# The low half of the FFN's gate and up weights by an adding DMA instead of a VectorE subtraction

## The chip, the cores and the metric

The kernel runs on one core of a Trainium2 chip. The metric is the time of one launch on the device, in microseconds (us). The matrix engine is called PE, the vector engine DVE, the scalar engine ACT, the GpSimd engine POOL and the sync engine SP. SP issues nearly all of the DMAs; POOL issues a few, on a queue of its own.

## The reference

Two layers over 512 tokens of 1024 features, in float32. Each layer has three attention mixers, a gated merge and an output projection, and then the part that the change touches, a SwiGLU feed-forward network (FFN) with 2816 hidden features:

```python
for l in range(DEPTH):
    mod = (cond @ w_ada[l] + b_ada[l]).reshape(b, 6, d)
    ...
    u = rms_norm(x, g_ffn[l]) * (1 + sc_f) + sh_f
    h = jax.nn.silu(u @ w_ffn_gate[l]) * (u @ w_ffn_up[l])
    x = x + gt_f * (h @ w_ffn_down[l])
return rms_norm(x, g_final)
```

`mod` is the modulation: six vectors per layer that come from the condition and the matrix `w_ada`.

## The kernel before

**Products in two halves.** Each float32 operand of a large product is cut into hi, which is the value rounded to the format of PE's faster products (`F32R`), and lo, which is the value minus hi. `mm3` then makes three matmuls: hi times hi, hi of the weight times lo of the activations, and lo of the weight times hi of the activations (lines 199, 200 and 201). A weight tile of 128 x 1024 holds eight chunks of 128 columns, so one unit of the FFN's first products is 24 matmuls of 128 x 512.

**The weights' way.** `LOADS` lists all weight tiles in the order of their use. `load` (line 150) fetches one into a buffer `wraw` by a DMA from SP; there are four of these buffers. `divide` makes `wh` by ACT (line 171) and `wl` by DVE (line 173). `W` hands PE its unit, lets `divide` run three units ahead of it and `fetch` four in the FFN. There are three buffers each for `wh` and `wl`, and from the output projection to the end of the FFN a fourth (tag `x`). A `wraw` buffer can be loaded anew when the last instruction that reads it is through.

**The first products of the FFN** ("gu" units: gate and up in turn, 44 tiles a layer). The first three units are computed together in half the tokens and then in the other half (PSUM tiles `f`), since the norm of the second half comes later. After that each pass `f` has one gate unit (PSUM tile `fg`, three banks) and one up unit (`fu`, two banks), and then ACT makes `g` = silu(`fg`), DVE multiplies it by `fu` (line 894), ACT rounds that to `hh` (line 243) and DVE makes `hl` (line 244).

**The modulation in the background.** In layer 0's FFN each pass also works on two columns of the next layer's modulation: `background(2)` calls `ada` twice, and each loads 512 KB of `w_ada` into a `wraw` buffer, the same four that the weights use, and reduces it on DVE (line 372). Layer 1's FFN has none of this.

**Order.** PE issues in the order in which the program is written; the order on ACT, DVE, POOL and SP is made by a scheduler when the kernel is built, and each engine then works strictly in that order. SP's queue is one of them: a DMA that must wait for its buffer holds up all that stand behind it.

Of the kernel before, what the change touches and what calls it, by code (L numbers as in the profile page):

```python
# [17 lines left out]
P = 128  # L18
# [14 lines left out]
# columns of the constants  # L33
C_INV, C_SGN, C_N = 0, 1, 2
# columns of the small vectors of a layer
# [4 lines left out]
# the blocks of queries whose weights ScalarE normalises  # L40
SCALE_ACT = {"f": (3,), "m": (2, 3)}
# between steps of the products: scores of a head (c), and transposes and products of the head before (p)
# [8 lines left out]
# products of constants that keep TensorE's clock up at the start  # L51
WARM = (24, 12)
# steps of products before each norm of the latents
WAIT = (8, 3, 8, 4)
# the chunk after which the rope tables are made
ROPE_AT = 4
# the chunk of the first products of the FFN after which the second half's norm comes
SS_AT = 3
# how far the work of attention goes before other work in the schedule, and steps by which the weights' division waits
HP, LAG = 30, 1  # L60

# 2*pi in parts of 8 bits, so that a product with a whole number below 2**16 is exact
# [4 lines left out]
def tile_hybrid_trunk(ctx: ExitStack, tc: tile.TileContext, xT, cvec, pos, cst, cmask, vec, gfin,  # L67
# [19 lines left out]
    # TensorE issues in the order written here; the other engines as the scheduler finds best  # L87
    ctx.enter_context(tc.manual_schedule(engines={pe.engine}))

    # ScalarE's functions, in phases of one table set each  # L90
# [15 lines left out]
    def windows(l):  # L106
        """Units of matrix products to run beside the attention of a pair of heads."""
        fox = [[("proj", l, 3 * p + i) for i in range(3)] for p in range(4)]
        sb = [[("proj", l, 12 + 3 * p + i) for i in range(3)] for p in range(4)]
        mla = [[("uqr", l, p // 2)] * (p % 2 == 0) + [("uq", l, p), ("ukv", l, p)] for p in range(4)]  # L110
        mg = [("merge", l, b, m) for b in range(3) for m in range(KC)]
        w = fox + [mla[0], mla[1] + [sb[0][0]], mla[2] + [sb[0][1]], mla[3] + [sb[1][0]], [sb[0][2], sb[1][1]]]
        w.append([mg[0], sb[1][2], mg[1], mg[2]])
        for p in range(2, 4):
            w.append([u for i in range(3) for u in (mg[3 * p - 3 + i], sb[p][i])])
        return w + [mg[9:14], mg[14:16], mg[16:]]
# [42 lines left out]
    def divide(want, after=None):  # L159
        """hi and lo of the weights before the want-th; after: what goes before them on ScalarE and VectorE"""  # L160
        while len(splits) < min(want, len(LOADS)):
            j = len(splits)
            fetch(j + 1)
            c = LOADS[j][2]
            p_, tag = wp, ""
            if fourth[0]:
                fourth[1] += 1
                if fourth[1] % 4 == 1:
                    p_, tag = fourth[0], "x"
            wh = p_.tile([P, D], F32R, tag="wh" + tag, name="wh")  # L170
            ins = [act.copy(wh[:, :c], raws[j][:, :c]).ins]  # L171
            wl = p_.tile([P, D], F32R, tag="wl" + tag, name="wl")
            ins.append(dve.tensor_sub(wl[:, :c], raws[j][:, :c], wh[:, :c].bitcast(F32)).ins)  # L173
            for i, a in zip(ins, after or ()):
                tc.add_manual_dep(i, a.name, order, reason="more urgent")
            splits.append((wh, wl))

    def W(unit, n=1, raw=3, ready=2, lag=0):
        """The next n weights, of that unit on, as (hi, lo); later ones are on their way."""
        i = at[0]  # L180
        if fourth[0]:
            raw, ready = 4, 3
        assert LOADS[i][0] == unit, (LOADS[i][0], unit)
        at[0] = i + n
        divide(i + n)

        def ahead():
            divide(i + max(n, ready + 1))
            fetch(i + max(n, raw + 1))

        if lag:
            later(lag, ahead)
        else:
            ahead()
        return splits[i] if n == 1 else splits[i : i + n]

# [6 lines left out]
    def gemm(o, wt, acts, m=P, start=True, stop=True, c0=0, cols=FULL):  # L203
        """o += W^T a over the chunks of acts, in steps; wt = (hi, lo) holds them m columns each from c0 on."""
        wh, wl = wt
        n = len(acts)
        for k, (ah, al) in enumerate(acts):
            cs = slice(c0 + k * m, c0 + (k + 1) * m)
            mm3(o, wh[:, cs], wl[:, cs], ah[:, cols], al[:, cols], start and k == 0, stop and k == n - 1)
            if k < n - 1:  # L210
                yield
# [12 lines left out]
    def steps(n):  # L224
        """n steps of the products in the queue"""
        for _ in range(n):
            while queue:
                try:
                    next(queue[0])
                    break  # L230
                except StopIteration:
                    queue.pop(0)
            else:
                return
            tick()
# [14 lines left out]
    H = S // 2  # L250

    class Norm:
        """1/sqrt(mean of squares over the features) of half the tokens, in every partition."""
# [77 lines left out]
    make_identity(nc, identf)  # L331
    # additive masks of the diagonal block: a query sees keys <= it, and keys < it
# [9 lines left out]
    # rope tables, rows alike in each 32: cos, and -sin | +sin  # L342
# [9 lines left out]
    # sin: +-r; cos: sin(pi/2 - |r|)  # L352
# [10 lines left out]
    def ada(l, i, c, wt=None, on_pool=False, after=None):  # L363
        """Column c of part i of the modulation."""
# [12 lines left out]
        if i in (1, 4):  # L377
            # g * (1 + scale)
            s1, g0 = (s1a, V_GM) if i == 1 else (s1f, V_GF)
            dve.scalar_tensor_tensor(s1[l][:, c : c + 1], m, 1.0, vecs[:, l, g0 + c : g0 + c + 1], ALU.add, ALU.mult)  # L380
# [14 lines left out]
    # ================= layers =================  # L395
    def values(ap, psv, name, got):
        """[2 heads' features, tokens] in PSUM -> [keys, block, head, hi | lo of the features]."""
# [14 lines left out]
    class Head:  # L412
# [4 lines left out]
        def S(self, i):  # L417
# [8 lines left out]
            if self.kind == "s":  # L426
                # sigmoid(z) of the key times the product of sigmoid(-z) over the later keys
# [20 lines left out]
        def T(self, js):  # L448
            """The weights of key blocks js, keys on the partitions, as hi and lo."""
# [12 lines left out]
        def PV(self, j):  # L462
            """[64 features, queries] += values^T weights^T; rows 0-63: hi of the values, rows 64-127: lo."""
# [12 lines left out]
    def slot(cur, prev, n):  # L476
        """The scores of a head and the rest of the head before it, between n steps of the queue."""
# [13 lines left out]
    for l in range(L):  # L491
# [32 lines left out]
        if l == 0:  # L524
# [4 lines left out]
            def warm(n):  # L529
                """Products of constants while there is nothing else: TensorE's clock falls when it idles."""  # L530
# [5 lines left out]
            # room that has no other use yet  # L536
# [65 lines left out]
        # of a head: qa = its queries' hi and lo, ka = its keys' hi twice; kb = its keys' lo  # L602
# [80 lines left out]
        def latent_keys(pr):  # L683
            """The rows that are alike in all heads"""
# [57 lines left out]
        def merge(u, b, m):  # L742
            """merged[m] += sigmoid(gate) * (y_b w_o)"""
# [32 lines left out]
        # the first pair's projections, with the forget gates and the norms of the latents  # L776
        enqueue(0)
        steps(1)
        with scoped(f"fg{l}", "right") as lp:
            # log of the forget gates: min(z, 0) - ln(1 + exp(-|z|)); its sums, negated  # L780
# [183 lines left out]
def _inputs(x, c, positions, g_mix, w_ada, b_ada, w_in, b_fox_f, g_mla_q, w_mla_uq, g_mla_kv,  # L964
            w_mla_ukv, w_o_fox, w_o_mla, w_o_sb, w_out, g_ffn, w_ffn_gate, w_ffn_up, w_ffn_down, g_final):
    """The arrays of the launch: the inputs, laid out for it."""
# [5 lines left out]
    def tiles(w):  # L972
        # [L, K, N] -> [L, N / 128, 128 rows of a chunk, chunks, 128]
# [6 lines left out]
    def col(v):  # L980
        # [L, n * 128] -> [128, L, n]
        return v.reshape(v.shape[0], -1, P).transpose(2, 0, 1)
# [5 lines left out]
    def qkv(w):  # L988
        # q, k, v tiles of a pair of heads, pair after pair
# [9 lines left out]
    # l kc p quad head part 32 -> l quad p part kc head 32  # L999
    uqr = uqr.reshape(L, 3, P, 2, 4, 2, 32).transpose(0, 3, 2, 5, 1, 4, 6).reshape(L, 2, P, 768)  # L1000
    ukv = np.asarray(w_mla_ukv).reshape(L, 2, P, 4, 2, 2, 64)  # l kc p pair head k|v 64
    ukv = ukv.transpose(0, 3, 2, 5, 1, 4, 6).reshape(L, 4, P, 512)

    wo = np.stack([np.asarray(w_o_fox), np.asarray(w_o_mla), np.asarray(w_o_sb)], axis=1)  # L 3 512 1024
# [15 lines left out]
    # row i: queries of the first half of block i; keys of its second half  # L1020
# [25 lines left out]
# 10000 ** (-i / 16) in float32  # L1046
# [25 lines left out]
```

## Time and profile before

| what | us |
|---|---|
| median of 2 runs | 1899.68 (1897.41 and 1901.94) |
| span of the profiled execution | 1895.3 |
| PE busy | 1857.2 |
| DVE busy | 1169.2 |
| ACT busy | 852.1 |
| POOL busy | 141.8 |

The span runs from the first to the last instruction of one profiled execution, and what the metric adds to it is the start and the end of the launch: here the median of the runs lies 4.4 us above it. Layer 0's first FFN products run from about 595 to 841 us of the span, layer 1's from about 1521 to 1764 us. "Busy" of PE is modelled from pipelined matmuls, so 98% busy is not a PE at its peak, but idle time of PE that the profile shows is real.

### The profile page before, as it was taken

The page shows a single profiled execution, that of the slowest core. Times are in us where ns is not written, and L with a number is a line of the kernel's source. Part 1 is how long each engine was busy: PE and PEld are TensorE (multiplying, and loading weights), DVE is VectorE, ACT ScalarE, POOL GpSimd, SP SyncE. Part 2 cuts the span into 40 slices and gives each one's busy share as a digit, 9 for nine tenths or more (in the row PEclk, how much of TensorE's full clock was granted, in tenths as well). Part 3 has the DMA queues.
Part 4 walks back from the last instruction along what each step waited for, and adds up shares of the span by engine and source line. Part 5 has one row for each costly group of instructions (what it writes and reads, how often), then busy time and mean ns, then how long its engine had stood idle before and what let it go on. Part 6 is the DMA issues. An engine that isn't in the chain of part 4 may idle for free.

```text
span 1895.3 us, 24083 instructions
## 1 busy us (share of the span) xinstructions
PE 1857.2 (98%) x8956; PEld 1515.1 (80%) x8956; DVE 1169.2 (62%) x2043; ACT 852.1 (45%) x1543; POOL 141.8 (7%) x260
## 2 busy tenths in 40 slices
PE   6999999999999999999999999999999999999998
PEld 4788787777889888778897887777788888888887
DVE  8888887677756655554558898666664463333333
ACT  4767874443334322232237688544433342232321
POOL 4122100001000000000002121000110000000000
PEclk8999999999999999999999999999999999999999
DMA  7423323333642655555633222122142222223231
GB/s 276 141 73 81 82 79 117 102 110 131 208 150 70 211 177 184 171 184 194 197 107 101 66 68 85 66 84 83 68 145 99 97 100 100 95 95 98 92 92 53
DMA packets 76741, 224.22 MB, mean 118 GB/s; under 512 B 10768, under 2 KB 13968, under 8 KB 76624
## 3 DMA queue, kind: packets, MB, share of 16 engines
q1 hardware_dynamic: 69136, 213.30, 33.8%
q0 software_dynamic: 7488, 9.38, 2.5%
q8 instruction: 71, 1.16, 0.3%
q14 instruction: 46, 0.38, 0.1%
HBM read 209.20 MB, written 4.19 MB: 113 GB/s over the span
## 4 chain that ended last, share of the span: by engine, by line
PE 79%; DMA 9%; DVE 7%; issue 3%; ACT 2%; SPq 0%; DVEq 0%; POOL 0%; POOLq 0%
DMA wraw<-in_w_ada_dram 8%; PE gate L199 5%; PE gate L201 5%; PE gate L200 5%; PE proj L199 4%; PE proj L200 4%; PE dn L200 4%; PE dn L199 4%; PE dn L201 4%; PE proj L201 4%; PE o L199 3%; PE o L200 2%; PE o L201 2%; PE fu L200 2%; PE fu L199 2%
## 5 line engine op out<-in xcount | busy, mean ns | idle before, releaser
L171 ACT CAST wh<-wraw 128x1024 fp32r<-128x1024 f32 (+4 forms) x332 | 311.4, 939 | 560.3 <-PE fu L200 125.1
L173 DVE TENSOR_TENSOR wl<-wraw,wh 128x1024 fp32r<-128x1024 f32 (+4 forms) x332 | 375.8, 1132 | 230.0 <-ACT wh L171 224.7
L372 DVE CUSTOM_DVE_ANT_0 wraw<-wraw,condb 128x1024 f32<-128x1024 f32 x80 | 98.6, 1232 | 153.0 <-DMA wraw<-in_w_ada_dram 152.9
L199 PE MATMUL proj<-uh,wh 128*128 128x512 f32 x384 | 162.2, 422 | 0.0
L199 PE MATMUL gate<-uh,wh 128*128 128x512 f32 x384 | 157.8, 411 | 0.0
L201 PE MATMUL proj<-uh,wl 128*128 128x512 f32 x384 | 151.3, 394 | 0.0
L200 PE MATMUL proj<-ul,wh 128*128 128x512 f32 x384 | 151.3, 394 | 0.0
L201 PE MATMUL gate<-uh,wl 128*128 128x512 f32 x384 | 150.6, 392 | 0.0
L200 PE MATMUL gate<-ul,wh 128*128 128x512 f32 x384 | 150.6, 392 | 0.0
L199 PE MATMUL dn<-hh,wh 128*128 128x512 f32 (+1 forms) x396 | 145.5, 367 | 0.0
L200 PE MATMUL dn<-hl,wh 128*128 128x512 f32 (+1 forms) x396 | 145.4, 367 | 0.0
L201 PE MATMUL dn<-hh,wl 128*128 128x512 f32 (+1 forms) x396 | 144.4, 365 | 0.1
L201 PE MATMUL fu<-uh,wl 128*128 128x512 f32 x336 | 131.5, 391 | 1.6 <-DVE wl L173 1.6
L200 PE MATMUL fu<-ul,wh 128*128 128x512 f32 x336 | 131.0, 390 | 0.0
L199 PE MATMUL fu<-uh,wh 128*128 128x512 f32 x336 | 130.9, 389 | 0.0
L199 PE MATMUL fg<-uh,wh 128*128 128x512 f32 x320 | 125.5, 392 | 0.0
L200 PE MATMUL fg<-ul,wh 128*128 128x512 f32 x320 | 125.5, 392 | 0.0
L201 PE MATMUL fg<-uh,wl 128*128 128x512 f32 x320 | 125.5, 392 | 0.0
L199 PEld LDWEIGHTS gate<-uh,wh 128*128 128x128 f32 x384 | 72.0, 188 | 19.8 <-issue 4.8
L201 PEld LDWEIGHTS proj<-uh,wl 128*128 128x128 f32 x384 | 72.3, 188 | 16.9
L201 PEld LDWEIGHTS gate<-uh,wl 128*128 128x128 f32 x384 | 72.0, 188 | 16.7
L201 PEld LDWEIGHTS dn<-hh,wl 128*128 128x128 f32 x396 | 74.4, 188 | 13.3 <-DVE wl L173 0.5
(370 smaller groups left out, 3973.2 us busy)
## 6 DMA issues: line engine op xcount, KB each, us to landing
wraw<-in_w_proj_dram SPq DMA_DIRECT2D x96, 512.0 KB, 3.5
wraw<-in_w_gu_dram SPq DMA_DIRECT2D x88, 512.0 KB, 3.6
wraw<-in_w_ada_dram SPq DMA_DIRECT2D x80, 512.0 KB, 3.3
wraw<-in_w_dn_dram SPq DMA_DIRECT2D x32, 512.0 KB, 4.0
wraw<-in_w_o_dram SPq DMA_DIRECT2D x48, 256.0 KB, 2.6
wada<-in_w_ada_dram SPq DMA_DIRECT2D x16, 512.0 KB, 5.6
wraw<-in_w_out_dram SPq DMA_DIRECT2D x16, 512.0 KB, 3.5
wraw<-in_w_dn_dram SPq DMA_DIRECT2D x16, 384.0 KB, 3.1
```

The lines of the kernel that those rows point to most:

```text
L171: ins = [act.copy(wh[:, :c], raws[j][:, :c]).ins]
L173: ins.append(dve.tensor_sub(wl[:, :c], raws[j][:, :c], wh[:, :c].bitcast(F32)).ins)
L199: pe.matmul(o, wh, ah, start=start, stop=False)
L200: pe.matmul(o, wh, al, start=False, stop=False)
L201: pe.matmul(o, wl, ah, start=False, stop=stop)
L372: ins = dve.tensor_tensor_reduce(out=wt, in0=wt, in1=condb, op0=ALU.mult, op1=ALU.add, scale=1.0, scalar=0.0, accum_out=m).ins
```

## The change

For "gu" units alone, `wl` is no longer a subtraction on DVE. ACT writes minus the rounded weight into `wl` (a copy with scale -1, which rounds as the copy to `wh` does), and then a DMA issued from POOL adds the raw weight to what stands in `wl`. All other weights keep DVE's subtraction. Comments are taken out as well, which shifts lines behind the change by five.

```diff
             wl = p_.tile([P, D], F32R, tag="wl" + tag, name="wl")
-            ins.append(dve.tensor_sub(wl[:, :c], raws[j][:, :c], wh[:, :c].bitcast(F32)).ins)
+            if LOADS[j][0][0] == "gu":
+
+                act.activation(wl[:, :c], raws[j][:, :c], AF.Copy, scale=-1.0)
+                pool.dma_start(out=wl[:, :c], in_=raws[j][:, :c], accum_op=ALU.add)
+            else:
+                ins.append(dve.tensor_sub(wl[:, :c], raws[j][:, :c], wh[:, :c].bitcast(F32)).ins)
             for i, a in zip(ins, after or ()):
```

The scheduler also moves other instructions. On DVE, in layer 0's FFN, one pass stands like this before, from one multiplication of `g` to the next; `wraw...condb` is the reduction of a column of the modulation:

```order
L894 TENSOR_TENSOR g_6540<-g_6540,fu_6507 128x512
L372 ISA wraw_6624,mod1_81<-wraw_6624,condb_69 128x1024
L372 ISA mod1_81 128x1
L244 TENSOR_TENSOR hl6_6539<-g_6540,hh6_6538 128x512
L173 TENSOR_TENSOR wl_6558<-wraw_6512,wh_6556 128x1024
L376 TENSOR_TENSOR mod1_81<-mod1_81,vecs_70 128x1
L380 SCALAR_TENSOR_TENSOR s1a1_83<-mod1_81,vecs_70 128x1
L372 ISA wraw_6629,mod1_81<-wraw_6629,condb_69 128x1024
L372 ISA mod1_81 128x1
L173 TENSOR_TENSOR wl_6589<-wraw_6560,wh_6587 128x1024
```

The same pass on DVE now (the lines of the kernel are five higher):

```order
L899 TENSOR_TENSOR g_6557<-g_6557,fu_6523 128x512
L249 TENSOR_TENSOR hl6_6556<-g_6557,hh6_6555 128x512
L377 ISA wraw_6643,mod1_81<-wraw_6643,condb_69 128x1024
L377 ISA mod1_81 128x1
L381 TENSOR_TENSOR mod1_81<-mod1_81,vecs_70 128x1
L385 SCALAR_TENSOR_TENSOR s1a1_83<-mod1_81,vecs_70 128x1
L377 ISA wraw_6648,mod1_81<-wraw_6648,condb_69 128x1024
L377 ISA mod1_81 128x1
```

The two subtractions are gone, and `hl` stands ahead of both reductions instead of between them.

SP's queue has the same DMAs in the same order, gate, up and two columns of the modulation in each pass, but waits for other things. Before (what stands in brackets is awaited: `DVE` and `Activation` for an instruction of that engine, `DMAHW` for a DMA from SP):

```order
L150 DMA wraw_6560<-in_w_gu_dram 128x1024 [waits DMAHW6_49,DVE_49,Activation_49]
L150 DMA wraw_6591<-in_w_gu_dram 128x1024 [waits DVE_49]
L150 DMA wraw_6624<-in_w_ada_dram 128x1024 [waits DMAHW7_49,DMAHW1_49,DVE_49]
L150 DMA wraw_6629<-in_w_ada_dram 128x1024 [waits DMAHW0_49,DVE_49]
L150 DMA wraw_6639<-in_w_gu_dram 128x1024 [waits DMAHW2_49,DVE_49,Activation_49]
```

And now (`DMASW` is a DMA from POOL, here an adding one):

```order
L150 DMA wraw_6578<-in_w_gu_dram 128x1024 [waits DMAHW6_49,DMASW5_49,Activation_49]
L150 DMA wraw_6610<-in_w_gu_dram 128x1024 [waits DVE_49]
L150 DMA wraw_6643<-in_w_ada_dram 128x1024 [waits DMAHW1_49,DMAHW7_49,DMASW6_49,Activation_49]
L150 DMA wraw_6648<-in_w_ada_dram 128x1024 [waits DMAHW0_49,DVE_49]
L150 DMA wraw_6659<-in_w_gu_dram 128x1024 [waits DMAHW2_49,DMASW7_49,Activation_49]
```

The gate's load and the first column's load of each pass now wait for an adding DMA where they waited for a subtraction; the other two wait for a reduction on DVE as before.

On ACT, at the start of the first products, the units behind the first stand like this before (`sq` belongs to the norm, `uh` are the modulated activations):

```order
L171 CAST wh_5898<-wraw_5678 128x1024
L260 ACTIVATE sqnf0b_5798<-x1_2_4948 128x256
L285 ACTIVATE uh0_86<-v_5863,mod0_80 128x256
L285 ACTIVATE uh1_87<-v_5867,mod0_80 128x256
L171 CAST wh_5904<-wraw_5902 128x1024
L260 ACTIVATE sqnf0b_5827<-x1_3_4949 128x256
L285 ACTIVATE uh2_88<-v_5871,mod0_80 128x256
L285 ACTIVATE uh3_89<-v_5875,mod0_80 128x256
L171 CAST wh_5910<-wraw_5908 128x1024
```

And now:

```order
L171 CAST wh_5899<-wraw_5679 128x1024
L265 ACTIVATE sqnf0b_5799<-x1_2_4948 128x256
L290 ACTIVATE uh0_86<-v_5864,mod0_80 128x256
L290 ACTIVATE uh1_87<-v_5868,mod0_80 128x256
L175 ACTIVATE wl_5901<-wraw_5679 128x1024
L171 CAST wh_5906<-wraw_5904 128x1024
L265 ACTIVATE sqnf0b_5828<-x1_3_4949 128x256
L290 ACTIVATE uh2_88<-v_5872,mod0_80 128x256
L290 ACTIVATE uh3_89<-v_5876,mod0_80 128x256
L175 ACTIVATE wl_5908<-wraw_5904 128x1024
L171 CAST wh_5913<-wraw_5911 128x1024
```

Each unit has the second copy (line 175) behind its first one, with two `uh` between them.

## The prediction

> **What bounds the kernel now.** I read the page's first part, then the windows of the two stretches in which the change acts, then waits and chain there.
>
> ```profile
> span 1895.3 us, 24083 instructions
> PE 1857.2 (98%) x8956; PEld 1515.1 (80%) x8956; DVE 1169.2 (62%) x2043; ACT 852.1 (45%) x1543; POOL 141.8 (7%) x260
> ```
>
> PE bounds the kernel: it is idle for 1895.3 - 1857.2 = 38 us in all, so no relief of DVE can bring more than that, and what it brings must be PE idle time in the FFN. Windows of layer 0's first products, and of layer 1's:
>
> ```profile
> 630.00:700.00 70.00, 70.00 (x308) 57.42 (x307) 38.41 (x69) 19.88 (x26) 0.00 (x0) 1.00 0.56 186
> 1600.00:1700.00 100.00, 100.00 (x439) 82.08 (x438) 34.71 (x38) 29.38 (x38) 0.00 (x0) 1.00 0.27 95
> ```
>
> The columns are span of the window, busy PE, weight load, DVE, ACT, POOL, granted clock, DMA share and GB/s. In layer 1, 439 matmuls take 100 us, so a pass of 48 takes PE 48 x 100 / 439 = 10.93 us (a unit 5.47). PE has no idle time in either window, at full clock. What waits in layer 0 (microseconds in total, times, longest):
>
> ```profile
> DVE wraw L372 <- DMA wraw<-in_w_ada_dram: 97.4, 37, 5.5
> ...
> ACT wh L171 <- PE fu L200: 45.8, 14, 3.9
> ...
> PE fu L201 <- DVE wl L173: 1.6, 4, 0.7
> ```
>
> PE waits 1.6 us for the subtraction that the change removes, so that is about the whole prize there. But DVE waits 97.4 us for columns of the modulation, and the chain (start, duration, what) and SP's queue show why:
>
> ```profile
> 710.18 4.61 DMA wraw<-in_w_ada_dram
> ...
> 714.92 1.23 DVE wraw L372
> ...
> 716.18 3.13 DMA wraw<-in_w_ada_dram
> ...
> 720.49 1.22 DVE L173 TENSOR_TENSOR wl<-wraw,wh 128x1024 fp32r<-128x1024 f32 x1
> 720.60 0.33 SPq L150 DMA_DIRECT2D wraw<-in_w_gu_dram  x1
> 721.74 0.33 SPq L150 DMA_DIRECT2D wraw<-in_w_ada_dram  x1
> ```
>
> Four `wraw` buffers carry four loads a pass, and make a ring: column 1 lands, is reduced, column 2 takes its buffer, lands at 719.3, is reduced, frees the up unit's load (720.60), and column 1 of the next pass goes out when the subtraction that ends at 721.7 frees its buffer. One turn is 721.74 - 710.18 = 11.56 us, longer than PE's 10.93. DVE works in order, so `g` falls behind PE:
>
> ```profile
> 640.53 0.69 DVE L894 TENSOR_TENSOR g<-g,fu 128x512 f32<-128x512 f32 x1 [2.04 <-PE fu L201]
> ...
> 839.77 0.69 DVE L894 TENSOR_TENSOR g<-g,fu 128x512 f32<-128x512 f32 x1
> 840.86 0.40 PE L199 MATMUL dn<-hh,wh 128*128 128x512 f32 x1
> ```
>
> At 640 DVE still waits for PE; the multiplication at 839.77 belongs to the pass that PE ended one pass before 840.86, at 829.9, and is 9.9 us late. PE feels lateness only at 16.4 us: `fu` has two banks, so the up unit of pass f+2 needs the multiplication of pass f, and starts 10.93 + 5.47 us after that pass ended. The kernel before ends the stage just inside this room.
>
> **The change, part by part.** Removed: 88 subtractions of 1.22 us on DVE, of which PE waited for next to nothing. Added: 88 copies of 1.05 us on ACT (as the cast below), which is busy 19.88 of 70 us there, so they cost only where PE waits for the weight. And 88 adding DMAs of 512 KB on POOL's queue; POOL is busy 0.00 there, so nothing stands before them. PE's wait moves from DVE to that DMA, and the buffer is held until it lands.
>
> *The price of an adding DMA.* The trace has none. The nearest rows are the shares of the two queues and two kinds of DMA (KB, median us to landing):
>
> ```profile
> q1 hardware_dynamic: 69136, 213.30, 33.8%
> q0 software_dynamic: 7488, 9.38, 2.5%
> wraw<-in_w_gu_dram SPq DMA_DIRECT2D x88, 512.0 KB, 3.6
> t<-t POOLq DMA_DIRECT2D x32, 128.0 KB, 2.3
> ```
>
> For 512 KB (0.524 MB) a load of SP occupies the 16 engines 0.338 x 1895.3 x 0.524 / 213.3 = 1.57 us, a copy of POOL's queue 0.025 x 1895.3 x 0.524 / 9.38 = 2.65 us. An addition reads two operands for one write. The lower bound is a load's 1.57 us, the upper twice POOL's copy, 5.3 us; I take twice a load, 3.15 us, which also lies nearest POOL's own copy. A POOL copy of 128 KB lands in 2.3 us, of which 2.65 / 4 = 0.66 is engine time, so 1.64 is fixed: an adding DMA lands in 1.64 + 3.15 = 4.8 us (bounds 3.2 and 6.9) after its copy on ACT.
>
> The Trainium skill, page "Collectives: The Full Stack", Part 3, says that a reduce in the DMA engines costs two source reads and no more, so about half of 31 GB/s an engine. For 32 KB an engine that is an estimate of 2.1 us; by it the sum below would be about 20 us and the change within 2%. No run here shows an adding DMA yet; this trace's loads (1.57 us) run near 21 GB/s an engine, slower than the page's 31.
>
> *The start of the first products, both layers.* PE needs three units at once, in buffers that it frees only as the output projection ends:
>
> ```profile
> 589.59 1.03 ACT L171 CAST wh<-wraw 128x1024 fp32r<-128x1024 f32 x1
> 590.84 0.89 ACT L285 ACTIVATE uh<-v,mod 128x256 fp32r<-128x256 f32 x2
> 592.17 1.05 ACT L171 CAST wh<-wraw 128x1024 fp32r<-128x1024 f32 x1 [0.44 <-PE wout L200]
> 594.92 1.15 DVE wl L173
> 596.07 0.04 issue
> 596.11 0.39 PE f L201
> 1520.93 1.15 DVE wl L173
> 1522.08 0.04 issue
> 1522.12 0.38 PE f L201
> ```
>
> PE takes the third unit's lo at 596.11, the moment that DVE has made it, and likewise at 1522.12. In ACT's new order the third unit's second copy ends, from 589.59, after two casts (2.1), two squares (0.7), two pairs of `uh` (1.6) and two copies (2.1): 596.1. The DMA then lands 4.8 us later. All of it is new PE idle time: **4.8 us a layer**. Next, the unit behind these is split when the three are through:
>
> ```profile
> 612.22 1.05 ACT L171 CAST wh<-wraw 128x1024 fp32r<-128x1024 f32 x1 [2.66 <-PE f L200]
> 613.17 0.59 ACT L101 ACTIVATE g<-f 128x512 f32<-128x512 f32 x1
> 618.77 0.39 PE L201 MATMUL fg<-uh,wl 128*128 128x512 f32 x1
> ```
>
> Cast, silu, second copy: 612.22 + 2.7 = 614.9, plus 4.8 is 619.7, where PE wants it at 618.77: **0.9 us a layer**. Later units are split about three units ahead (16 us), which covers 2.1 + 4.8. Both places in both layers: 2 x 5.7 = **11.4 us** (bounds 6.4 and 20).
>
> *The ring in layer 0.* The new turn no longer has the subtraction (11.56 - 1.2 = 10.3), but column 1 then goes out right behind the up unit's load instead of 1.1 us after it and lands behind it on the same queue, so I count half of the gain away: 10.9, PE's own pace. Onto that comes contention: two adding DMAs bring 2 x 3.15 = 6.3 us of engine time a pass, the engines are already 0.56 busy, and the ring's two loads are in flight 8.2 of 10.9 us. If packets of the two queues alternate, half of the overlapping time is lost: 6.3 x 0.75 / 2 = 2.4. One turn is 13.3 us, 2.4 more than PE's pass. Over 20 passes DVE falls 47 us behind, 16.4 of which the banks take: **31 us** of PE idle time (with 1.57 us: turn 12.1, 7 us; with 5.3 us: turn 14.9, 63 us). Layer 1 has two loads a pass and no ring, and loses nothing in its passes while the adding DMA costs under (10.93 - 2 x 1.57) / 2 = 3.9 us of engine time.
>
> *Sum:* 11.4 + 31 = 42 us on the span of 1895.3, and as much on the median of 1899.7, which stands 4.4 above: **1942 us**.
>
> **Rivals.** *The additions are hidden* (the other side: not slower). A turn up to 10.93 + 16.4 / 20 = 11.75 us is taken by the banks over 20 passes; below that layer 0's passes cost nothing, and only the starts remain, 6 to 11 us: 1906 to 1911. For it: engines half idle, and the subtraction out of the ring. Against: the ring is at 11.56 already, and the buffer of column 1 now waits for a DMA. It decides at about 1.6 us of contention-free engine time, the lower bound. The skill's page "DMA: Bandwidth & Descriptors", section on the anatomy of a SWDGE DMA, gives 2.0 us plus bytes over 436 GB/s, an estimate of 3.2 us to landing here, which would be this rival; it is stated for copies, and the trace's 128 KB copies (2.3 us) agree with it within 0.1.
>
> *The addition is far slower than two reads*, at the upper bound of 5.3 us or more. Then the engines bound both layers: a pass of layer 0 needs 4 x 1.57 + 10.6 = 16.9 us, of layer 1 2 x 1.57 + 10.6 = 13.7. That is 20 x 6 - 16 = 104 and 20 x 2.8 - 9 = 47 (9 us being the slack of a unit split 16 us ahead), with the starts 170 us: 2070; at 4.5 us about 2000. Against: a load's packets show no such rate.
>
> *DVE's relief opens the ring*: turn 10.3, `g` on time, PE's 1.6 and the waits of 0.2 at the starts come back, and the adding DMA lands early enough: 1897, no change. Against: the lo of the third unit is waited for to the moment.
>
> That the change does not do what it says is out: DVE's rows have lost the subtractions.
>
> **How the numbers follow.** Forecast (turn 12.3 to 14.5, 1922 to 1985) 0.58, of which 0.41 above 1938 and 0.17 below; hidden 0.25; far slower 0.15; relief 0.02. Two per cent of 1899.7 is 38 us, about what a measurement of this kernel can tell from no change. Slower by over 2%: 0.41 + 0.15 = 0.56; faster by as much 0.01, since PE's idle time forbids it; within 0.43. The range takes in the hidden case's 1906 and half of the far slower: 1906 to 2030. The forecast alone: 1922 to 1985.
>
> **What the new profile would show.** Right: PE `f` waiting about 5 us for a DMA `wl` at the start of both first products; `g` in layer 0 at intervals over 12.5 us, PE `fu` waiting for it in the second half of the stage; layer 1 at 10.93. Wrong: intervals below 11.8 (hidden), layer 1 over 10.93 with PE waiting for `wl` in each pass (far slower). The sum hangs on the engine time of an adding DMA, which the share of queue q0 will show.

## The result, and the profile after

| | before | after |
|---|---|---|
| median, us | 1899.68 (1897.41 and 1901.94) | 1951.81 (1951.75 and 1951.87) |
| span of the profiled execution, us | 1895.3 | 1950.0 |
| PE busy, us | 1857.2 | 1873.2 |

The changed kernel takes 1.028 times as long (95% interval 1.026 to 1.030), 52 us more. The forecast was 1942, in a range of 1906 to 2030.

The page of the changed kernel, busy times first, then the shares of the two DMA queues, then two kinds of DMA (KB each, median us to landing):

```profile
PE 1873.2 (96%) x8956; PEld 1522.4 (78%) x8956; DVE 1072.3 (55%) x1955; ACT 932.6 (48%) x1631; POOL 218.7 (11%) x348
...
q1 hardware_dynamic: 69136, 213.30, 33.6%
q0 software_dynamic: 20160, 55.52, 15.6%
...
wraw<-in_w_gu_dram SPq DMA_DIRECT2D x88, 512.0 KB, 5.0
wl<-wraw POOLq DMA_DIRECT2D x88, 512.0 KB, 6.1
```

DVE lost 97 us of work and it bought nothing. The same 8956 matmuls take PE 16.0 us longer, and its idle time grew from 1895.3 - 1857.2 = 38.1 to 76.8 us, 38.7 more. Queue q0 holds the additions: 0.156 x 1950.0 = 304.2 us, less the 0.025 x 1895.3 = 47.4 that it carried before, over 88 is **2.92 us of engine time for one addition**. Loads of the weights land 1.4 us later than before (3.6).

Where the time went is seen by stage. Stages are cut at the first matmul of `f`, of `fu` and of `dn`, read from the timelines of both kernels (us):

| stage | before | after | more |
|---|---|---|---|
| start of layer 0's first products (`f`) | 18.0 | 25.4 | 7.4 |
| layer 0's passes | 228.0 | 264.2 | 36.2 |
| start of layer 1's first products | 18.0 | 25.1 | 7.1 |
| layer 1's passes | 224.9 | 225.9 | 1.0 |

That is 51.7 of the 54.7 us between the spans. The rest is a layer 0 whose first products begin 1.6 us earlier, an end that is 4.3 us longer, and 0.3 us elsewhere. Of the end: from the last matmul to the end of the span there are 8.2 us before and 12.5 after. What differs is POOL's closing DRAIN. It begins 1.0 us after the last matmul in both, and is the longest of three (ns: shortest, median, longest), first before, then now:

```profile
L1059 POOLq DRAIN  x3: 40/93/3492, 1888.0 to 1895.0; - x3
...
L1064 POOLq DRAIN  x3: 40/93/10720, 1938.5 to 1949.7; - x3
```

Its length goes with the DMAs that POOL has issued in the launch: with 140, 180, 184, 220 and 228 of them it takes 3.5, 6.8, 7.1, 10.0 and 10.7 us in the kernels of this document, 0.082 us for each one more, in experiment 11 (10.7) with copies that add nothing. Experiment 6 alone, with two additions to one tile, does not fit (228 and 7.9 us). So these 4.3 us come with the 88 new DMAs, although no product waits for them; what the DRAIN does in that time no run shows.

Waits of PE in the changed kernel (us in total, times, longest):

```profile
PE fg L206 <- DMA wl<-wraw: 21.2, 13, 2.4
PE f L206 <- DMA wl<-wraw: 10.1, 4, 3.0
PE fu L206 <- DMA wl<-wraw: 3.7, 7, 0.8
PE fu L204 <- DVE g L899: 3.6, 2, 2.3
```

Four waits of `f`, two in each layer, are the starts. Layer 0's, on the timeline:

```profile
593.05 1.04 ACT L175 ACTIVATE wl<-wraw 128x1024 fp32r<-128x1024 f32 x1
...
594.39 0.86 POOL L176 DMA_DIRECT2D wl<-wraw  x1 [2.12 <-ACT wl L175]
...
596.02 0.38 PE L206 MATMUL f<-uh,wl 128*128 128x256 f32 x1 [2.04 <-DMA wl<-wraw]
...
599.64 0.58 PE L206 MATMUL f<-uh,wl 128*128 128x256 f32 x1 [3.00 <-DMA wl<-wraw]
```

The third unit's second copy ends at 594.1, its addition is issued at 594.39 and lands 5.2 us later, when PE goes on; the wait before is for the second unit's. PE waited 2.04 + 3.00 = 5.0 us; the stage grew by 7.4, and the windows behind the wait say why (start and end, length, PE busy, granted clock, DMA share, GB/s):

```profile
598.00:602.00 4.00, 2.36 (x11) 0.50 0.99 242
602.00:606.00 4.00, 4.00 (x24) 0.66 0.80 215
606.00:610.00 4.00, 4.00 (x36) 1.00 0.22 84
```

The granted clock is 0.50 around the wait and 0.66 in the next window, which has 24 matmuls in 4 us where 36 fit four us later.

In layer 0's passes PE is no longer full, and in layer 1's it is (length, then PE, weight load, DVE, ACT, POOL, clock, DMA share, GB/s):

```profile
630.00:700.00 70.00, 68.04 (x297) 55.05 (x296) 23.57 (x50) 25.88 (x31) 8.71 (x10) 1.00 0.96 260
700.00:770.00 70.00, 61.22 (x247) 47.57 (x246) 21.06 (x44) 25.95 (x32) 8.71 (x10) 0.95 0.86 232
...
1600.00:1700.00 100.00, 100.00 (x439) 82.10 (x438) 12.43 (x18) 46.04 (x55) 15.69 (x18) 1.00 0.88 206
```

Layer 1 has two additions a pass as layer 0 has, the DMA engines are 0.88 busy, and PE runs its 439 matmuls as before. The chain in layer 0 (start, duration, what) shows what layer 1 lacks:

```profile
766.46 5.46 DMA wraw<-in_w_ada_dram
...
772.13 1.23 DVE wraw L377
...
773.40 5.68 DMA wraw<-in_w_ada_dram
...
779.10 1.23 DVE wraw L377
...
780.86 5.24 DMA wraw<-in_w_ada_dram
```

A pass is still two columns of the modulation one after the other: column 1 lands, is reduced, column 2 is loaded, lands, is reduced, and then the next pass's column 1 is loaded. This turn takes 780.86 - 766.46 = 14.40 us. The two landings are 5.46 and 5.68 us, where the turn shown of the kernel before had 4.61 and 3.13. That PE falls behind can be read from `g` on DVE:

```profile
668.27 0.69 DVE L899 TENSOR_TENSOR g<-g,fu 128x512 f32<-128x512 f32 x1
...
875.51 0.69 DVE L899 TENSOR_TENSOR g<-g,fu 128x512 f32<-128x512 f32 x1
```

There are 15 passes between these two, 13.82 us each.

How the late columns reach PE is seen on SP, ACT, POOL and PE:

```profile
760.08 0.33 SPq L150 DMA_DIRECT2D wraw<-in_w_ada_dram  x1
...
760.51 0.39 SPq L150 DMA_DIRECT2D wraw<-in_w_gu_dram  x1
...
766.77 0.62 ACT L248 CAST hh<-g 128x512 fp32r<-128x512 f32 x1 [7.31 <-DVE g L899]
...
768.61 1.05 ACT L171 CAST wh<-wraw 128x1024 fp32r<-128x1024 f32 x1 [1.23 <-DMA wraw<-in_w_gu_dram]
...
770.91 0.87 POOL L176 DMA_DIRECT2D wl<-wraw  x1 [10.29 <-ACT wl L175]
...
776.38 0.50 PE L206 MATMUL fg<-uh,wl 128*128 128x512 f32 x1 [2.40 <-DMA wl<-wraw]
```

The gate unit's load stands on SP's queue behind column 2, which waits for the reduction of column 1. It goes out at 760.51 and lands at 768.5, 8.0 us later. ACT works in order and waits 7.31 us for `g`, but `hh` is through at 767.4, and the cast behind it waits 1.23 us more for that load. Then the second copy and the addition follow, and PE waits for the gate unit's lo. The load came last in this way in nine of the twelve waits of `fg` in layer 0's passes (18.0 of their 20.5 us), `hh` in two (1.8 us).

### The profile page after: what moved, and what is told of

Its sections match the earlier page's. It is cut to its first block, busy times and chain, and to the rows that moved or that the text cites. A ratio compares the mean times of both kernels' runs of the same rounds, so it can differ in the third digit from the quotient of the medians.

```text
span 1950.0 us, 24299 instructions
## 1 busy us (share of the span) xinstructions
PE 1873.2 (96%) x8956; PEld 1522.4 (78%) x8956; DVE 1072.3 (55%) x1955; ACT 932.6 (48%) x1631; POOL 218.7 (11%) x348
## 3 DMA queue, kind: packets, MB, share of 16 engines
q1 hardware_dynamic: 69136, 213.30, 33.6%
## 4 chain that ended last, share of the span: by engine, by line
PE 73%; DMA 12%; DVE 6%; issue 5%; ACT 2%; SPq 0%; POOL 0%; DVEq 0%; POOLq 0%; ACTq 0%
DMA wraw<-in_w_ada_dram 9%; PE gate L204 5%; PE gate L206 4%; PE gate L205 4%; PE proj L204 4%; PE dn L205 4%; PE dn L204 4%; PE dn L206 4%; PE proj L205 4%; PE proj L206 4%; PE o L204 2%; PE o L205 2%; PE o L206 2%; DVE wraw L377 2%; PE fg L206 2%
## 5 line engine op out<-in xcount | busy, mean ns | idle before, releaser
L178 DVE TENSOR_TENSOR wl<-wraw,wh 128x1024 fp32r<-128x1024 f32 (+4 forms) x244 | 268.2, 1100 | 153.6 <-ACT wh L171 150.5
L176 POOL DMA_DIRECT2D wl<-wraw x88 | 76.7, 872 | 648.8 <-ACT wl L175 448.9
L206 PE MATMUL fg<-uh,wl 128*128 128x512 f32 x320 | 128.6, 402 | 21.2 <-DMA wl<-wraw 21.2
L899 DVE TENSOR_TENSOR g<-g,fu 128x512 f32<-128x512 f32 x42 | 28.9, 687 | 158.3 <-PE fu L206 150.9
L248 ACT CAST hh<-g 128x512 fp32r<-128x512 f32 x44 | 26.9, 612 | 138.8 <-DVE g L899 138.8
L175 ACT ACTIVATE wl<-wraw 128x1024 fp32r<-128x1024 f32 x88 | 92.8, 1054 | 0.0
```

Source lines behind the costliest of these rows:

```text
L175: act.activation(wl[:, :c], raws[j][:, :c], AF.Copy, scale=-1.0)
L176: pool.dma_start(out=wl[:, :c], in_=raws[j][:, :c], accum_op=ALU.add)
L206: pe.matmul(o, wl, ah, start=False, stop=stop)
L248: act.copy(h, src)
L899: dve.tensor_mul(g, g, t2)
```

## Experiments

Four readings were to be told apart: **A**, the DMA engines' time per pass is the bound in layer 0; **C**, ScalarE's extra copies are; **D**, the traffic of the additions lengthens the landing of the columns, of which two stand in series; **B** or **H**, an addition holds the load's buffer too long, or lands too late. The kernel before was timed beside each group; its medians were 1898.3, 1899.3 and 1898.9 us.

**1. Layer 1 alone** (a unit is `("gu", layer, number)`)**.**

```diff
-            if LOADS[j][0][0] == "gu":
+            if LOADS[j][0][0] == "gu" and LOADS[j][0][1] == 1:
```

> Adding DMAs in layer 1's first products alone; layer 0 subtracts on VectorE as before. Theory A (in layer 0 the DMA engines have four loads of 1.57 us and two additions of about 2.9 us a pass, more than PE's 10.93): only layer 1's start, which stands 7.1 us longer in the changed kernel's trace, and its 0.9 us of passes remain, so about 1908 us, and layer 0's g at 11.56 us or under as before. Theory B (the loss is the landing time of an addition, 6 us, wherever it stands): layer 1 has the same additions and the same landing time, so half of the 52 us, about 1925.

Measured 1908.1 us (1.0052, 1.0037 to 1.0067). The start of layer 1 takes 25.0 us, its passes 225.9; layer 0's passes take 229.6 us (228.0 before). Layer 1's 44 additions cost 10 of the 52 us, and those of layer 0 the rest, so it isn't the landing time wherever it stands.

**2. The first four units of each layer subtracted on VectorE.**

```diff
-            if LOADS[j][0][0] == "gu":
+            if LOADS[j][0][0] == "gu" and LOADS[j][0][2] >= 4:
```

> The first four units of each layer by VectorE's subtraction, the other 80 by adding DMAs. Theory A (two separate losses: 7.4 and 7.1 us at the two starts, 36 us in layer 0's passes): the start of first products falls back to 18.2 us in both layers and 14 to 15 us come back, about 1937 us. Theory B (the late start is what makes layer 0's passes late): the passes mend too, under 1920 us.

Measured 1939.1 us (1.0221, 1.0200 to 1.0241). Both starts are 18.0 us again, and layer 0's passes stay long, 267.6 us in the profiled execution, which was the slowest of four (1945.3). The two losses are separate.

**3. A copy instead of an addition.**

```diff
-                pool.dma_start(out=wl[:, :c], in_=raws[j][:, :c], accum_op=ALU.add)
+                pool.dma_start(out=wl[:, :c], in_=raws[j][:, :c])
```

> The DMA copies the weight into lo instead of adding it (leaves out the subtraction, so lo is the whole weight): same bytes read from SBUF by POOL's queue, but one read instead of two. Theory A (engine time decides): a copy's engine time was put at 2.65 us from the 128 KB copies, so 4 x 1.57 + 2 x 2.65 = 11.6 us a pass at 0.93 busy is 12.5, layer 0 loses 15 us and the starts about 10: 1925 us, and queue q0's share falls from 0.156 to about 0.14. Theory B (the way through POOL's queue costs, whatever the operation): within 5 us of 1952.

Measured 1926.6 us (1.0150, 1.0135 to 1.0166). Here lo is the whole weight. The sum came out and its terms did not. Of that kernel's page:

```profile
q0 software_dynamic: 20160, 55.52, 9.1%
...
wl<-wraw POOLq DMA_DIRECT2D x88, 512.0 KB, 4.0
```

(0.091 x 1923.7 - 47.4) / 88 = 1.45 us of engine time: an addition costs two copies, 2.92 to 1.45. Layer 0's passes take 233.7 us (5.7 more than before, not 15), but the two starts 25.8 and 25.4, as long as with additions, and the end is as long too. The copy lands in 2.9 us in the quiet of layer 1, but the third unit's goes out at 596.08 beside a load, behind ACT's second copy, and takes 5.7 us; PE waits 5.1 us for it.

**4. No DMA.**

```diff
                 act.activation(wl[:, :c], raws[j][:, :c], AF.Copy, scale=-1.0)
-                pool.dma_start(out=wl[:, :c], in_=raws[j][:, :c], accum_op=ALU.add)
```

> ScalarE's second copy stays, the adding DMA is left out, so lo stays minus the weight. Theory A (the DMA's engine time and landing are the whole loss): as the kernel before or a little under, 1893 to 1902 us. Theory C (ScalarE, in order, is late through 88 copies of 1.05 us, and its casts and hh with it): a third or more of the 52 us remains, 1917 us or more, with PE waiting for ScalarE's wh or wl.

Measured 1894.4 us (0.9977, 0.9967 to 0.9986). The passes take 224.9 us in both layers. ACT's 88 copies cost nothing that shows, and C is out. Without anything to wait for, a launch would be 4 us shorter than before: that is all that the subtractions on DVE cost.

**5. Up units alone, after the start.**

```diff
-            if LOADS[j][0][0] == "gu":
+            if LOADS[j][0][0] == "gu" and LOADS[j][0][2] >= 4 and LOADS[j][0][2] % 2 == 1:
```

> Adding DMAs for the up units alone, and not for the first four units of a layer: 40 instead of 88. Theory A (in layer 0 the DMA engines' time decides: an addition takes 2.92 us of all sixteen, a load 1.57): a pass of layer 0 needs 4 x 1.57 + 2.92 = 9.2 us, under PE's 10.93, so next to nothing is lost, 1898 to 1905 us. Theory B (landing time in the ring of four buffers decides): the gate unit's load still waits for the buffer of an up unit, which is held until an addition lands, so about half of layer 0's 36 us stays, 1915 us or more.

Measured 1945.7 us (1.0243, 1.0223 to 1.0262): A fails, and B named the direction but not the size. With less than half of the additions layer 0's passes take 272.5 us, more than with all of them, while the engines have room:

```profile
640.00:840.00 200.00, 173.46 (x715) 138.31 (x714) 73.11 (x138) 58.04 (x72) 13.00 (x15) 0.96 0.67 187
```

A is out as an explanation here. The timeline shows the turn (`x2` and its duration stand for two DMAs issued behind each other):

```profile
766.32 0.33 SPq L150 DMA_DIRECT2D wraw<-in_w_ada_dram  x1
...
772.40 1.23 DVE L377 CUSTOM_DVE_ANT_0 wraw<-wraw,condb 128x1024 f32<-128x1024 f32 x1 [5.31 <-DMA wraw<-in_w_ada_dram]
...
773.55 1.22 DVE L178 TENSOR_TENSOR wl<-wraw,wh 128x1024 fp32r<-128x1024 f32 x1
...
774.80 6.25 SPq L150 DMA_DIRECT2D wraw<-in_w_ada_dram  x2
...
779.45 1.23 DVE L377 CUSTOM_DVE_ANT_0 wraw<-wraw,condb 128x1024 f32<-128x1024 f32 x1 [4.02 <-DMA wraw<-in_w_ada_dram]
```

One column lands beside the up unit's addition (in 6.1 us), the other without one (4.5), and the gate unit's subtraction stands between a reduction and the next load. `g` follows every 14.0 to 14.6 us there. The chain kept the subtraction that the changed kernel takes out of it, and has one of its two landings lengthened.

**6. A second addition behind each, layer 1 alone.** The condition is that of experiment 1, and a second DMA follows:

```diff
+                pool.dma_start(out=wl[:, :c], in_=condb[:, :c], accum_op=ALU.add)
```

> Adding DMAs in layer 1 alone, and behind each a second one that adds another tile of SBUF to the same lo (so the output isn't the reference's). Theory A (engine time): a pass of layer 1 needs 2 x 1.57 + 4 x 2.92 = 14.8 us instead of 9.0, over PE's 10.93, so about 20 x 3.9 = 78 us less some 10 of cover, and 5 more at the start: 1975 to 1985 us, with g in layer 1 at 14.8 us or more. Theory B (landing time alone): two additions land in about 12 us, within the 16 us by which a unit is split ahead, so only the start grows: 1913 to 1920 us.

Measured 2062.6 us (1.0860, 1.0844 to 1.0876), neither. Layer 1's passes take 369.6 us, 18.0 each, with the engines 0.79 busy. POOL's waits in 300 us of it:

```profile
POOL wl L177 <- DMA wl<-wraw: 232.7, 32, 7.6
```

The second addition writes the same tile and waits on POOL for the first to land, 7.3 us each time, and the next unit's first addition is queued behind it. The kernel made a chain on POOL, so it tells A and B apart badly. It shows that POOL's order turns a landing time into a pace: 9.0 us a unit.

**7. No columns.** Layer 1's modulation is set to zero instead of being loaded and reduced:

```diff
-        wt = wt or load(w_ada[l, j])
+        wt = wt or (load(w_ada[l, j]) if l == 0 else None)
         m = mods[l][:, j : j + 1]
-        if on_pool:
+        if l == 1:
+            ins = dve.memset(m, 0.0).ins
+        elif on_pool:
```

> All additions stay; the loads and reductions of the columns of layer 1's modulation, which run beside layer 0's FFN, are left out (set to zero). Theory A: a pass of layer 0 has 2 x 1.57 + 2 x 2.92 = 9.0 us of engine time, PE keeps 10.93 as in layer 1, and only the two starts (7.4 and 7.1 us) and about 1 us in each layer's passes remain: 1910 to 1917 us. Theory C (the additions cost by themselves in layer 0, through POOL's queue or ScalarE): 1930 us or more.

Measured 1919.6 us (1.0110, 1.0093 to 1.0128). The starts are 25.4 and 25.1 us, layer 0's passes 227.6 with 869 matmuls in the 200 us from 640 on. All 88 additions are there; without the columns (the last eight of layer 0's own are still reduced, until 674) they cost nothing in the passes. What the expectation lacks lies ahead of the FFN, where layer 0's first products begin 2.5 us later than before, and at the end, 4.3 us.

**8. The columns in two buffers of their own,** in the room of the fourth pair of hi and lo.

```diff
-                if fourth[1] % 4 == 1:
+                if False:
...
+        if fourth[0] and not wt:
+            wt = fourth[0].tile([P, D], F32, tag="wcol", bufs=2, name="wcol")
+            nc.sync.dma_start(out=wt, in_=w_ada[l, j])
         wt = wt or load(w_ada[l, j])
```

> The columns of the modulation get two buffers of their own in the FFN (in the room of the fourth pair of hi and lo, which is left out there), so no column waits for an addition to free a buffer; the same DMAs run. Theory A (engine time): 4 x 1.57 + 2 x 2.92 = 12.1 us a pass stay, PE still loses most of layer 0's 36 us: 1940 us or more. Theory B (the shared ring of four buffers is what is late): layer 0's passes are back within 8 us of 227.9 us: 1915 to 1925 us. Layer 1, without columns, shows what three pairs of hi and lo instead of four cost by themselves.

Measured 1961.6 us (1.0333, 1.0314 to 1.0352), and inconclusive: with three pairs the first products began 12.3 us later and their starts took 31.9 and 30.2 us, and the columns, free of the ring, ran ahead and were done by 710 us. From there the passes of layer 0 take 10.88 us; over the whole stage 243.6.

**9. One column in a pass.** The columns left over run in layer 1.

```diff
                 gated(t, t2)
-                background(2)
+                background(1)
```

> The changed kernel with one column of the next layer's modulation in a pass of layer 0 instead of two; the columns left over run in layer 1, where the same list is worked off. Theory D (layer 0's pass is a chain of two columns one after the other: two landings of 5.1 us, two reductions of 1.23 us and about 1 us): with one column in a pass the chain has one landing less, PE keeps 10.93 us, and only the two starts remain with a microsecond or two: 1912 to 1920 us. Theory A (engine time): 3 x 1.57 + 2 x 2.92 = 10.5 us a pass, 11.3 at 0.93 busy, which two banks would also just take. Theory C (additions cost in layer 0 whatever the columns do): over 1930 us.

Measured 1915.4 us (1.0083, 1.0068 to 1.0098). All additions and all columns are there. Layer 0's passes take 225.9 us:

```profile
640.00:840.00 200.00, 200.00 (x876) 164.23 (x875) 49.76 (x98) 91.70 (x108) 31.39 (x36) 1.00 0.92 234
```

PE is full with the engines 0.92 busy, and a column takes 8.6 us to land there. A long landing is no loss when the chain has only one.

**10. The addition reads hi,** so the load's buffer is free after ACT's two copies. Minus hi plus hi leaves lo at zero, and not with the wrong sign, as the expectation has it.

```diff
-                pool.dma_start(out=wl[:, :c], in_=raws[j][:, :c], accum_op=ALU.add)
+                pool.dma_start(out=wl[:, :c], in_=wh[:, :c], accum_op=ALU.add)
```

> The adding DMA adds hi instead of the weight (leaves lo with the wrong sign): same traffic, same landing, but the load's buffer is free after ScalarE's two copies and isn't held until the addition lands. Theory D (the additions lengthen the landing of the columns, by traffic): layer 0's passes stay long, 1940 to 1955 us. Theory H (the buffer is held by the addition, and so the next load goes out late): most of layer 0's 36 us comes back, 1915 to 1925 us.

Measured 1930.3 us (1.0167, 1.0152 to 1.0182). Layer 0's passes fall to 230.6 us, 33.6 of their 36.2 come back, as H said; the total is above H's range since the starts grow to 28.5 and 29.1 us, and layer 0's last products and layer 1's passes by 2 to 3 us each, and the end is as long as in the changed kernel. The traffic is the same, and D alone falls:

```profile
640.00:840.00 200.00, 199.34 (x869) 162.60 (x869) 71.10 (x153) 88.51 (x104) 30.66 (x36) 1.00 0.99 277
```

The engines are 0.99 busy and PE loses nothing. DVE shows why:

```profile
768.81 1.23 DVE L377 CUSTOM_DVE_ANT_0 wraw<-wraw,condb 128x1024 f32<-128x1024 f32 x1 [8.24 <-DMA wraw<-in_w_ada_dram]
...
771.17 1.22 DVE L377 CUSTOM_DVE_ANT_0 wraw<-wraw,condb 128x1024 f32<-128x1024 f32 x1 [0.33 <-DMA wraw<-in_w_ada_dram]
```

With buffers free, both columns of a pass are loaded side by side (each takes about 7 us), and DVE waits once, not twice. So in the changed kernel the additions hold the buffers and thereby keep the columns in series.

**11. Traffic alone.** The kernel before, with two copies of hi to DRAM for each unit of layer 0 that nothing waits for.

```diff
+    junk = nc.dram_tensor("junk", (2, 2 * NF, P, D), F32).ap()
...
+            if LOADS[j][0][0] == "gu" and LOADS[j][0][1] == 0:
+                for i in range(2):
+                    pool.dma_start(out=junk[i, LOADS[j][0][2]][:, :c], in_=wh[:, :c].bitcast(F32))
```

> The kernel before, VectorE's subtraction included, with two plain DMAs of hi to a scratch in DRAM for each unit of layer 0's first products on POOL's queue (two copies were 2 x 1.45 us of engine time, an addition 2.92): nothing waits for them, and they hold no buffer of a load. Theory D (traffic): columns land in about 5 us instead of 4, a pass of layer 0 takes 13 to 13.5 us, and 20 to 36 us are lost: 1920 to 1936 us. Theory H (holding and waiting): at most 1905 us.

Measured 1962.9 us (1.0332, 1.0313 to 1.0350): D's direction, and nearly twice its size. The starts are as before, layer 0's passes take 289.8 us. In the chain the landings are longer while the subtractions stay in it:

```profile
767.91 5.04 DMA wraw<-in_w_ada_dram
...
773.08 1.23 DVE wraw L376
...
780.84 5.38 DMA wraw<-in_w_ada_dram
...
787.62 6.92 DMA wraw<-in_w_ada_dram
```

Here no addition holds a load's buffer, and the copies, which read hi, do not hold ACT up either (between 640 and 840 its casts wait for loads alone, 8.1 us). So H alone falls as well. The copies took (0.090 x 1961.1 - 47.4) / 88 = 1.47 us of engine time each, two of them an addition's.

**12. One column in a pass, and the start on VectorE.** Experiments 2 and 9 together.

> One column in a pass, and the first four units of each layer subtracted on VectorE. If the two losses are the starts and the chain of two columns, both are gone: 1896 to 1904 us, no measurable difference from the kernel before. If a third cost of the additions is left, over 1910 us.

Measured 1901.1 us (1.0011, 1.0002 to 1.0020). The starts are 18.0 us, the passes 227.1 and 225.9. The expectation is met. No third cost is left in the products; the end, 3.6 us longer by POOL's DRAIN after 80 more DMAs, is the only stage that grew by more than 1.0 us. Nothing is won over the kernel before either: PE is the bound.

The 200 us from 640 on, in layer 0's passes, side by side. PE at its full pace does 876 matmuls; "landing" is the median time in which a column of the modulation lands:

| kernel | matmuls | DMA share | landing, us | columns in series in a pass |
|---|---|---|---|---|
| before | 863 | 0.54 | 4.3 | 2, and a subtraction |
| changed | 741 | 0.89 | 5.2 | 2 |
| 3, copies | 846 | 0.76 | 4.6 | 2 |
| 5, up units alone | 715 | 0.67 | 4.9 | 2, and a subtraction |
| 10, adds hi | 869 | 0.99 | 7.2 | side by side |
| 11, traffic alone | 657 | 0.82 | 5.6 | 2, and a subtraction |
| 9, one column | 876 | 0.92 | 8.6 | 1 |

The DMA share doesn't order the losses; the length of the chain's turn does. Read from the issue times of the columns in the same 200 us, a turn of two takes 11.0 us in 10, 11.8 before, 12.0 in 3, 13.5 in the changed kernel, 13.9 in 5 and 15.0 in 11, the order of the matmuls. The loss in layer 0's passes needs both of these at once: two columns in series on four buffers, and landings made longer by the additions. Each experiment that takes one away (4 and 3 the traffic, in whole or half; 7 and 9 a column; 10 the series) brings most of it back.

## Why the prediction was right

*The bound and the place.* The ring of two columns was named as what sets layer 0's passes, and the starts as the other place; experiments 2, 9 and 12 show that there are these two in the products and no third. The end of the launch, 4.3 us longer, is a place that was not named. Layer 1's passes cost 1.0 us, against the 0.9 of the unit behind its start.

*The price of an addition* was put at 3.15 us, bounded by 1.57 and 5.3. It is 2.92. The way there was partly luck: the copies on POOL's queue before, of 128 KB and less, taken as 2.65 us for 512 KB, overstate a large copy, which takes 1.45 (experiment 3); what holds is that an addition costs twice a copy. The Trainium skill says of a reduce that it is slower by its two source reads ("Collectives: The Full Stack", Part 3), and the ratio of 2.0 agrees; its 31 GB/s an engine does not, since 32 KB in 1.45 us are 22.6 GB/s here. Landing was put at 4.8 us: it took 4.6 and 5.2 at the start, 6.1 in the median. The fit in the Trainium skill's page "DMA: Bandwidth & Descriptors", section on the anatomy of a SWDGE DMA, gave 3.2 us: copies in the quiet of layer 1 land in 2.9, additions in 6.2.

*The starts* were put at 4.8 us of waiting and 0.9 behind them, in each layer. PE waited 5.0 us. That this is so near is partly luck: the third unit's second copy ended at 594.1, not at the forecast's 596.1, but PE also reached these products 1.6 us earlier. The stages grew by 7.4 and 7.1, and the difference is a term that the sum did not have: the clock. By the records of the granted clock it stood at half for 6.8 us at each of the two starts, and for 3.4 us three times in layer 0's passes. At layer 0's start 5.1 of the 6.8 us lie behind the wait and cost half of that, 2.5 us, which is the difference. So the sum of 42 us was all idle time and had errors that partly cancel: PE's new idle time ahead of the end is 38.7 - 4.3 = 34.4 us, 8 less, and the sum had nothing for the 16.0 us by which PE is slower at the same matmuls or for the 4.3 us at the end. Half clock explains about 10 of the 16.0 (2 x 2.5 at the starts, 3 x 1.7 in the passes); where the rest comes from is open.

*The turn* was put at 13.3 us; `g` shows 13.8. Of the 14.4 us turn shown, the landings have 5.46 + 5.68, 3.4 us more than the 4.61 + 3.13 before; by the medians of the table it is 2 x 0.9 = 1.8. Contention was put at 2.4 us, plus half of a lost gain. Two numbers of the working do not follow: the ring's loads are in flight 4.61 + 3.13 = 7.7 us by its own chain, not 8.2, which makes contention 2.2 and the sum 3 us less; and a turn of 14.5 us gives 1966, not 1985, for which about 14.9 and the starts' upper bound are needed.

*How it reaches PE* failed. The step that lets `fu`'s two banks take 16.4 us of lateness, and then has PE wait for `g`, described the lesser part: that wait is 3.6 us in all. SP's queue came first: the gate unit's load stands behind the column that waits for the ring, lands late, is split late, and PE waits 21.2 us for its lo. The size came out by that other way, which is luck: 31 us of idle time forecast, 21.2 + 3.7 + 3.6 = 28.5 us of waits by the rows above (0.7 of them in layer 1), in a stage 36.2 us longer.

*The rivals.* "Hidden" needed a turn under 11.75 us and was out. "Far slower" needed engine time above 3.9 us. "Relief" is what experiment 4 shows with the addition left out: 1894 us. The remark that the sum hangs on the engine time was right only for this chain: experiment 10 hides the same additions in layer 0's passes with the engines 0.99 busy.

## What to carry to other kernels

Work that is moved to an idle-looking DMA engine costs its landing time in whatever chain runs through the same buffers, long before the engines are full; so count the loads that stand in series and what holds their buffers, not the share of busy time. Before an instruction is taken off an engine, read what waits for it: here PE waited 1.6 us for the subtractions in the passes, so no replacement could win more than a few microseconds. And where a wait of PE is forecast, add what PE loses at half clock behind it; where POOL issues many DMAs, add the longer end.

## What the runs showed of the hardware that was not expected

An adding DMA of 512 KB took 2.92 us of all sixteen engines and a plain copy of the same size 1.45; POOL spent 872 ns on issuing the one and 539 ns on the other. Each DMA that POOL had issued added 0.082 us to its DRAIN at the end of the launch (3.5 us after 140 of them, 10.7 after 228), which shows in the time where the DRAIN outlasts SP's last waits (7.5 us after the last matmul before and now).

PE's clock was granted at half after quite short waits. Behind the wait of 2.27 us that ended at 714.20, PE did 8 matmuls of 512 columns in 3.4 us; just before it did 14 in 3:

```profile
708.00:711.00 3.00, 3.00 (x14) 1.00 1.03 227
711.00:714.00 3.00, 0.94 (x5) 0.99 0.41 167
714.00:717.40 3.40, 3.20 (x8) 0.50 0.86 299
717.40:720.00 2.60, 2.60 (x13) 1.00 0.74 150
```

A wait of 2.40 us at 776.38 was not followed by a slower clock, so the length of a wait alone does not decide. The Trainium skill's page "TensorE: Matmul & The Clock Gate", Part 1, has the clock fall after at least one idle window of about 3.4 us: the slow stretches in the two FFNs last 3.41 us or twice that, which agrees with the window, but waits of 2.1 to 2.4 us, shorter than one, were enough three times in this kernel, and here the measurement decides.
